# MLA latents normed in one step and transposed by feature tile, mask rows with their zeros in one transfer

## The chip, the cores and the metric

The kernel runs on one NeuronCore of a Trainium2 chip. The metric is the device time of one execution in microseconds, the median of the runs shown. The names of engines in rows are PE (TensorE, matmuls) and PEld (its weight loads), DVE (VectorE), ACT (ScalarE), POOL (GpSimd) and SP (SyncE, which issues most transfers). Each engine works through its own queue of instructions in a fixed order and stops at an instruction whose inputs or buffers are not ready.

## What is computed

One layer of a streaming encoder on 512 tokens of width 1024. The input is normed and multiplied with `w_in`; the result feeds two mixers, a Mamba-2 scan (16 heads in 4 groups) and a multi-head latent attention (MLA, 16 heads). Their outputs go through `w_out`; a cross-attention to 256 memory tokens and a convolutional feed-forward block follow, and a final norm. The part that the change touches is the way from the latents to the attention:

```python
q_lat, kv_lat, k_rope = jnp.split(u, [384, 640], axis=-1)          # u: 512 x 672
q  = (rmsnorm(q_lat,  q_norm_w)  @ w_q_up ).reshape(b, s, 16, 96)  # 64 plain, 32 rotary
kv = (rmsnorm(kv_lat, kv_norm_w) @ w_kv_up).reshape(b, s, 16, 128) # 64 key, 64 value
k_rope = apply_rope(k_rope, cos, sin)
mask = k_chunk[None, :] <= q_chunk[:, None]                        # chunks of 64 tokens
```

## The kernel before

Tokens are tiled by 128, so there are four token tiles `t`. All matrix products run as three matmuls in float32r: operands are split into a high part and a residue (`split`: a cast on ScalarE, line 94, and a subtraction on VectorE, line 95; weight pages use lines 156 to 158, where GpSimd takes half of the residue), and `mm3` (lines 103 to 105) adds high x high, high x low and low x high in one PSUM bank. PSUM has three `acc` banks for products, two `tr` banks for transposes, two `s` banks and one `pv` bank.

`lat` holds, for each token tile, 16 columns of dt, 384 of q latents, 256 of kv latents and 32 of rotary key. Its first 256 columns are made at the start; `late_unit(t)` makes the other 432 for one token tile, copying the accumulator to `lat` on ScalarE (line 674).

The scan goes through `seq`, 16 pairs of head group and token tile, in three steps: `ssd_a` (decay matrix aE, its transfer from DRAM on GpSimd's queue, line 537, the masked C-B product `cbm`, line 541, and the split of M and xs), `ssd_b` (products, state S, output y, its own norm) and `ssd_d` (transposes of y). For the last head group the steps are written out as strings in `PLAN`, one for each token tile. Its letters: z, d, a, b are the gate unit and the scan's steps, l a late unit, i `lat_init`, q0 to q3 and k0 to k3 the norms of q and kv latents of one token tile, p1 to p3 one to three output parts, U the first q projection (`q_up`), s and S the set-up of the key and query tiles.

A norm, `lat_norm`, squares the latents of one tile on ScalarE with a row sum (line 619), scales the sum on VectorE (line 140), raises it to the power -0.5 on GpSimd (line 142), multiplies latents, this factor and the weight row into a buffer of its own on VectorE (line 621), transposes three or two 128x128 blocks on TensorE into one `tr` bank (line 119) and splits each block into the tiles `LT[k]` (shown as `lt` in rows; lines 94 and 95). `lat_kv` also rotates the tile's rotary key in four steps on VectorE (lines 635 to 638). `q_up` multiplies `LT[0]` to `LT[2]` with a page of `w_q_up`, copies to `qrow` (line 723) and rotates there in four products on GpSimd (lines 726 to 729); `v_up` and `k_pair` use `LT[3]` and `LT[4]`.

An output part (`out_part`, lines 646 to 660) is a 256-column product of the scan's finished half with `w_out`, 12 matmuls; it reads rows of x into one of five `xo` buffers and writes the sum to DRAM. Sixteen such parts need no latents; those not named in `PLAN` run inside the attention loop as fills. `setup_kq1` (lines 685 to 693) fills the four mask rows of the key and query tiles: a memset for the low half and a transfer on GpSimd's queue for the high half.

The program is built through a planner (`schedule_with_timeline_sim=True`): it takes the order in which the code is written as priority, orders the instructions of each engine by a simulated timeline and adds the waits. The order on an engine is then fixed, and it need not be the order of the code.

Of the kernel before, what the change touches and what calls it, by code (L numbers as in the profile page):

```python
# [11 lines left out]
ALU = mybir.AluOpType  # L12
# [19 lines left out]
FM = FF // P  # L32
MASK_NEG = -float(2 ** 100)

PLAN = ('z z z z d a l l b', 'l l d a i q0 k0 p1 q1 b p1 q2 k1 p1 q3 k2', 'p1 d a k3 p1 b p1', 'p1 d U p2 b p3 s S')


def shape_constants():
    t = np.arange(P)[:, None]
    l = np.arange(P)[None, :]  # L40
    cen = ((t > 63) & (t <= l)).astype(np.float32) - ((t > l) & (t <= 63))
    c = np.concatenate([t == l, t <= l, cen, t <= l, t > l, np.ones((P, P))], axis=1).astype(np.float32)
    m = np.zeros((NT, 2, T), np.float32)
    for j in range(NT):
        m[j, 0, j * P:j * P + 64] = 1.0
        m[j, 1, j * P + 64:(j + 1) * P] = MASK_NEG
    f = np.array([np.float32(1.0) / np.float32(np.float64(10000.0) ** np.float64(np.float32(i) / np.float32(ROPE)))
                  for i in range(0, ROPE, 2)], np.float32).reshape(1, ROPE // 2)
    return c, m, f
# [13 lines left out]
def tile_block(ctx, tc, x, mem, positions, norm_mix_w, w_in, ssd_conv_w, ssd_conv_b, ssd_dt_bias,  # L63
# [541 lines left out]
    def lat_init():  # L605
        LT.extend(k4([P, 2, T], "lt", F32R) for _ in range(3))
        LT.extend(page("lt") for _ in range(2))
        qkl = k4([P, 1024], "qkl")
        box["qw"], box["kvw"] = row_tile(qkl[:, 0:QR], mla_q_norm_w), row_tile(qkl[:, QR:QR + KVR], mla_kv_norm_w)
        box["ln"] = qkl[:, QR + KVR:]  # L610
        nc.vector.tensor_scalar(box["qw"], box["qw"], float(QH) ** -0.5, None, ALU.mult)
        x4 = k4([P, 4, 256], "xo")
        xo.extend(x4[:, i] for i in range(3))
        box["lnk"] = [gw[0], x4[:, 3]]

    def lat_norm(t, o, n, w, l0, l1, ln):
        ss = small([P, 1], "ssl", 2)
        src = lat[:, t, SSD_H + o:SSD_H + o + n]
        nc.scalar.activation(ln, src, AF.Square, accum_out=ss)
        rs = rstd_of(ss, n, "l")  # L620
        nc.vector.scalar_tensor_tensor(ln, src, rs, w, ALU.mult, ALU.mult)
        ps = tr_bank().rearrange("p (k t) -> p k t", k=4)
        for k in range(l0, l1):
            transpose(ps[:, k - l0], ln[:, tsl(k - l0)])
        for k in range(l0, l1):
            split(LT[k][:, 0, tsl(t)], LT[k][:, 1, tsl(t)], ps[:, k - l0])

    def lat_q(t):
        lat_norm(t, 0, QR, box["qw"], 0, 3, box["ln"])

    def lat_kv(t):
        lat_norm(t, QR, KVR, box["kvw"], 3, 5, box["lnk"][t % 2])
        kr = lat[:, t, SSD_H + QR + KVR:]
        tmp = small([P, ROPE], "krt", 1)
        nc.vector.tensor_tensor(tmp[:, 0:H2], kr[:, H2:], sinb[:, t, 0:H2], ALU.mult)
        nc.vector.tensor_tensor(tmp[:, H2:], kr[:, 0:H2], sinb[:, t, H2:], ALU.mult)
        nc.vector.tensor_tensor(kr, kr, cosb[:, t], ALU.mult)
        nc.vector.tensor_tensor(kr, kr, tmp, ALU.add)

    with tc.issue_after(last):  # L640
        for u, rows in xbc_units(0):
# [23 lines left out]
    def late_unit(t):  # L665
        n, c0 = LATW - 256, C_DT + 256
        if t == 0:
            late_pages.extend(wpage(w_in[0][2 * P * j:2 * P * (j + 1), c0:c0 + n].rearrange(
                "(k p) c -> p k c", p=P), 2, n) for j in range(4))
        acc = acc_bank()[:, :n]  # L670
        for k in range(KD):
            hi, lo = late_pages[k // 2]
            mm3(acc, (hT[0][:, k, tsl(t)], hT[1][:, k, tsl(t)]), (hi[:, k % 2], lo[:, k % 2]), k == 0, k == KD - 1)
        nc.scalar.copy(lat[:, t, 256:], acc)

    late = [lambda t=t: late_unit(t) for t in range(NT)]
    parts = [lambda i=i: out_part(0, i) for i in range(16)]
# [7 lines left out]
    def setup_kq1():  # L685
        for b in range(2):
            kt = k4([P, 2, T], f"kt{b}", F32R)
            qt = k4([P, 2, T], f"qt{b}", F32R)
            for i, (tl, w) in enumerate(((qt, masks[:, 0]), (kt, masks[:, 1]))):
                nc.vector.memset(f32(tl[QH:KROWS, 1]), 0.0)  # L690
                nc.gpsimd.dma_start(tl[QH:KROWS, 0], w)
            kts.append(kt)
            qts.append(qt)

# [142 lines left out]
    def do(op, i):  # L837
        g, c = seq[i]
        if op == "z":
            z_unit(g, zn.pop(0))  # L840
        elif op == "l":
            late.pop(0)()
        elif op == "d":
            ssd_d(*seq[i - 1])
        elif op == "a":
            ssd_a(*seq[i + 1])
        elif op == "b":
            ssd_b(g, c)
        elif op == "i":
            lat_init()  # L850
        elif op[0] == "q":
            lat_q(int(op[1]))
        elif op[0] == "k":
            lat_kv(int(op[1]))
        elif op[0] == "p":
            part(int(op[1]))
        elif op == "s":
            setup_kq1()
        elif op == "U":
            q_up(0)  # L860
        elif op == "S":
            setup_kq2()
# [364 lines left out]
```

## Time and profile before

| | us |
|---|---|
| median of 3 runs (987.09 to 988.03) | 987.62 |
| profiled execution | 987.27 |
| its span, first to last instruction | 985.5 |
| TensorE busy | 965.7 |
| VectorE busy | 662.1 |
| ScalarE busy | 523.4 |
| GpSimd busy | 279.6 |
| mean granted TensorE clock | 0.994 |

All rows come from one profiled execution. A busy time adds up the time in which an engine has an instruction running, so it says nothing on whether the time that is left hurts: for that, the stretches and waits of the engine that is busiest are read, here TensorE's. A granted clock of 1 is 2.4 GHz.

### The profile page before, as it was taken

The numbers are of one execution on the slowest core, as the hardware profiler recorded it, in microseconds if no ns is written. First come the engines' busy times: TensorE is split into PE (matmuls) and PEld (weight loads), VectorE is DVE, ScalarE is ACT, GpSimd is POOL, SyncE is SP. The second block draws the span as 40 slices with busy tenths as digits, with TensorE's granted clock in tenths as the row PEclk, the third lists the DMA queues.
The fourth block names the chain that finished last, engine by engine and source line by source line (L and its number), as shares of the span: only waits on it lengthen the run. The fifth ranks groups of instructions, "written<-read, shape, count | busy, mean of one in ns | idle before, by whom it ended". The sixth has DMA issues, their size and how long they took to land.

```text
span 985.5 us, 14980 instructions
## 1 busy us (share of the span) xinstructions
PE 965.7 (98%) x5385; PEld 843.0 (86%) x5385; DVE 662.1 (67%) x1210; ACT 523.4 (53%) x1078; POOL 279.6 (28%) x360
## 2 busy tenths in 40 slices
PE   8999999999999999999999999999999999999997
PEld 6889998898899999988888888888888888888886
DVE  5989999868779786773654435766667666722553
ACT  5677776655477677753544434444444444321442
POOL 2016547656653547452443222000000000000000
PEclk9999999999999999999999999999999999999999
DMA  7653432315423336242241120433223322332462
GB/s 242 208 175 95 116 108 77 97 49 179 155 78 103 113 113 233 86 155 80 86 150 65 65 86 22 128 107 107 86 87 108 105 85 93 113 116 97 156 223 80
DMA packets 90306, 114.07 MB, mean 116 GB/s; under 512 B 5799, under 2 KB 70119, under 8 KB 89848
## 3 DMA queue, kind: packets, MB, share of 16 engines
q1 hardware_dynamic: 88536, 106.78, 34.0%
q0 software_dynamic: 1696, 6.33, 2.1%
q8 instruction: 43, 0.70, 0.3%
q14 instruction: 31, 0.25, 0.1%
HBM read 104.67 MB, written 8.42 MB: 115 GB/s over the span
## 4 chain that ended last, share of the span: by engine, by line
PE 82%; DVE 7%; DMA 3%; ACT 3%; POOL 2%; issue 2%; SPq 0%; POOLq 0%; ACTq 0%; DVEq 0%
PE acc L103 22%; PE acc L105 22%; PE acc L104 22%; PE tr L119 3%; PE s L103 3%; PE s L105 3%; PE s L104 3%; PE pv L811 2%; DMA aE<-acT 2%; DVE wl L157 1%; ACT aE L544 1%; PE acc L119 1%; DVE cu L434 1%; DMA wr<-in_w_in_dram 1%; POOL xdD L550 1%
## 5 line engine op out<-in xcount | busy, mean ns | idle before, releaser
L103 PE MATMUL acc<-Ah,wh 128*128 128x512 f32 (+1 forms) x560 | 215.5, 385 | 0.2 <-ACT Ah L94 0.2
L104 PE MATMUL acc<-Al,wh 128*128 128x512 f32 (+1 forms) x560 | 215.4, 385 | 0.2 <-DVE Al L95 0.2
L105 PE MATMUL acc<-Ah,wl 128*128 128x512 f32 (+1 forms) x560 | 215.0, 384 | 0.0
L95 DVE TENSOR_TENSOR wl<-wr,wh 128x1024 fp32r<-128x1024 f32 (+1 forms) x99 | 120.0, 1213 | 101.6 <-ACT wh L94 100.9
L94 ACT CAST wh<-wr 128x1024 fp32r<-128x1024 f32 (+1 forms) x99 | 102.0, 1031 | 133.5 <-PE acc L104 63.7
L158 POOL TENSOR_TENSOR wl<-wr,wh 128x512 fp32r<-128x512 f32 (+2 forms) x64 | 103.5, 1625 | 86.2 <-ACT wh L156 79.8
L142 POOL TENSOR_TENSOR rs<-ms,neg_half 128x1 f32<-128x1 f32 x18 | 10.8, 600 | 409.5 <-DVE ms L140 397.9
L104 PEld LDWEIGHTS acc<-Al,wh 128*128 128x128 f32 x560 | 105.3, 188 | 20.3 <-DVE Al L95 0.5
L105 PEld LDWEIGHTS acc<-Ah,wl 128*128 128x128 f32 x560 | 105.3, 188 | 20.2
L103 PEld LDWEIGHTS acc<-Ah,wh 128*128 128x128 f32 x560 | 105.2, 188 | 20.0 <-ACT Ah L94 0.5
L156 ACT CAST wh<-wr 128x1024 fp32r<-128x1024 f32 (+2 forms) x64 | 65.4, 1029 | 40.1 <-PE s L105 10.7
L1121 DVE SCALAR_TENSOR_TENSOR cbuf<-acc,fcw,cbuf 128x511 f32<-128x511 f32 (+1 forms) x88 | 65.6, 747 | 26.6 <-ACT cbuf L1119 25.1
L157 DVE TENSOR_TENSOR wl<-wr,wh 128x512 fp32r<-128x512 f32 (+2 forms) x64 | 59.3, 932 | 35.7 <-ACT wh L156 34.7
L103 PE MATMUL acc<-wh,Ah 128*128 128x256 f32 (+2 forms) x240 | 77.2, 323 | 1.0 <-ACT Ah L94 1.0
L105 PE MATMUL acc<-wh,Al 128*128 128x256 f32 (+2 forms) x240 | 76.2, 319 | 0.0
L104 PE MATMUL acc<-wl,Ah 128*128 128x256 f32 (+2 forms) x240 | 75.9, 318 | 0.0
L795 POOL TENSOR_SCALAR p<-p,ri 128x128 f32<-128x128 f32 (+1 forms) x64 | 34.5, 542 | 71.7 <-DVE ri L794 71.1
L103 PEld LDWEIGHTS acc<-wh,Ah 128*128 128x128 f32 x240 | 46.1, 192 | 4.2 <-ACT Ah L94 1.4
L105 PEld LDWEIGHTS acc<-wh,Al 128*128 128x128 f32 x240 | 46.1, 192 | 2.6 <-DVE Al L95 0.3
L104 PEld LDWEIGHTS acc<-wl,Ah 128*128 128x128 f32 x240 | 46.2, 192 | 2.3
L1119 ACT ACTIVATE cbuf<-acc,fcb,fcw 128x512 f32<-128x512 f32 x44 | 34.3, 779 | 24.0 <-PE acc L105 24.0
L104 PE MATMUL acc<-wl,act 128*128 128x512 f32 (+1 forms) x112 | 40.5, 363 | 0.0
(370 smaller groups left out, 2349.3 us busy)
## 6 DMA issues: line engine op xcount, KB each, us to landing
wr<-in_w_ffn_up_dram SPq DMA_DIRECT2D x44, 512.0 KB, 3.5
wr<-in_w_ffn_down_dram SPq DMA_DIRECT2D x33, 512.0 KB, 3.3
wr<-in_w_in_dram SPq DMA_DIRECT2D x26, 512.0 KB, 3.9
wr<-in_w_out_dram SPq DMA_DIRECT2D x16, 512.0 KB, 3.5
aE<-acT POOLq DMA_DIRECT2D x16, 256.0 KB, 3.5
wr<-in_w_mem_k_dram SPq DMA_DIRECT2D x8, 512.0 KB, 4.5
wr<-in_w_mem_v_dram SPq DMA_DIRECT2D x8, 512.0 KB, 3.4
wr<-in_w_mem_q_dram SPq DMA_DIRECT2D x8, 512.0 KB, 3.6
```

The costliest lines, as they stand in the source:

```text
L94: first = nc.scalar.copy(hi, src)
L95: nc.vector.tensor_tensor(lo, src, f32(hi), ALU.subtract)
L103: nc.tensor.matmul(acc, lhsT=lh, rhs=rh, start=first, stop=False)
L104: nc.tensor.matmul(acc, lhsT=lh, rhs=rl, start=False, stop=False)
L105: nc.tensor.matmul(acc, lhsT=ll, rhs=rh, start=False, stop=last)
L119: nc.tensor.transpose(dst, src, ident[:n, :n])
L156: nc.scalar.copy(hi, raw)
L157: nc.vector.tensor_tensor(lo[:, 0:a // 2], raw[:, 0:a // 2], f32(hi[:, 0:a // 2]), ALU.subtract)
L158: nc.gpsimd.tensor_tensor(lo[:, a // 2:], raw[:, a // 2:], f32(hi[:, a // 2:]), ALU.subtract)
L795: nc.gpsimd.tensor_scalar(p_, p_, ri, 1.0, ALU.mult, ALU.mult)
L1119: nc.scalar.activation(u, acc, AF.Identity, scale=fcw[:, 2, m:m + 1], bias=fcb[:, m:m + 1])
L1121: nc.vector.scalar_tensor_tensor(u[:, s:], acc[:, :T - s], fcw[:, 2 - s, m:m + 1], u[:, s:], ALU.mult, ALU.add)
```

## The change

The latents' norm is one step `n` for all four token tiles. The squares move into `late_unit`, write their (unused) squares into the accumulator bank just copied from, and collect their eight row sums in one small tile `lss`; `n` scales the eight sums in two operations, takes one power on GpSimd, multiplies the latents in place in `lat`, and rotates all four tiles' keys in four operations. The transposes are steps `t0` to `t4`, one for each feature tile: four 128x128 blocks, one per token tile, into one bank, and one split of 512 columns. The buffers of the scaled latents go; `xo` gets a sixth buffer. The plan names one output part less. The masks carry the zero half, so the four memsets go and each transfer writes both halves. The space for descriptors of GpSimd's transfers is set to 8192 bytes per partition.

```diff
--- before.py
+++ after.py
@@ -32,7 +32,7 @@
 FM = FF // P
 MASK_NEG = -float(2 ** 100)
 
-PLAN = ('z z z z d a l l b', 'l l d a i q0 k0 p1 q1 b p1 q2 k1 p1 q3 k2', 'p1 d a k3 p1 b p1', 'p1 d U p2 b p3 s S')
+PLAN = ('z z z z d a l l b', 'l l d a i n b p1 t0 p1 t1 t2', 'p1 d a t3 p1 t4 b p1', 'p1 d U p2 b p3 s S')
 
 
 def shape_constants():
@@ -40,10 +40,10 @@
     l = np.arange(P)[None, :]
     cen = ((t > 63) & (t <= l)).astype(np.float32) - ((t > l) & (t <= 63))
     c = np.concatenate([t == l, t <= l, cen, t <= l, t > l, np.ones((P, P))], axis=1).astype(np.float32)
-    m = np.zeros((NT, 2, T), np.float32)
+    m = np.zeros((NT, 2, 2, T), np.float32)
     for j in range(NT):
-        m[j, 0, j * P:j * P + 64] = 1.0
-        m[j, 1, j * P + 64:(j + 1) * P] = MASK_NEG
+        m[j, 0, 0, j * P:j * P + 64] = 1.0
+        m[j, 1, 0, j * P + 64:(j + 1) * P] = MASK_NEG
     f = np.array([np.float32(1.0) / np.float32(np.float64(10000.0) ** np.float64(np.float32(i) / np.float32(ROPE)))
                   for i in range(0, ROPE, 2)], np.float32).reshape(1, ROPE // 2)
     return c, m, f
@@ -607,35 +607,35 @@
         LT.extend(page("lt") for _ in range(2))
         qkl = k4([P, 1024], "qkl")
         box["qw"], box["kvw"] = row_tile(qkl[:, 0:QR], mla_q_norm_w), row_tile(qkl[:, QR:QR + KVR], mla_kv_norm_w)
-        box["ln"] = qkl[:, QR + KVR:]
         nc.vector.tensor_scalar(box["qw"], box["qw"], float(QH) ** -0.5, None, ALU.mult)
         x4 = k4([P, 4, 256], "xo")
-        xo.extend(x4[:, i] for i in range(3))
-        box["lnk"] = [gw[0], x4[:, 3]]
-
-    def lat_norm(t, o, n, w, l0, l1, ln):
-        ss = small([P, 1], "ssl", 2)
-        src = lat[:, t, SSD_H + o:SSD_H + o + n]
-        nc.scalar.activation(ln, src, AF.Square, accum_out=ss)
-        rs = rstd_of(ss, n, "l")
-        nc.vector.scalar_tensor_tensor(ln, src, rs, w, ALU.mult, ALU.mult)
-        ps = tr_bank().rearrange("p (k t) -> p k t", k=4)
-        for k in range(l0, l1):
-            transpose(ps[:, k - l0], ln[:, tsl(k - l0)])
-        for k in range(l0, l1):
-            split(LT[k][:, 0, tsl(t)], LT[k][:, 1, tsl(t)], ps[:, k - l0])
-
-    def lat_q(t):
-        lat_norm(t, 0, QR, box["qw"], 0, 3, box["ln"])
-
-    def lat_kv(t):
-        lat_norm(t, QR, KVR, box["kvw"], 3, 5, box["lnk"][t % 2])
-        kr = lat[:, t, SSD_H + QR + KVR:]
-        tmp = small([P, ROPE], "krt", 1)
-        nc.vector.tensor_tensor(tmp[:, 0:H2], kr[:, H2:], sinb[:, t, 0:H2], ALU.mult)
-        nc.vector.tensor_tensor(tmp[:, H2:], kr[:, 0:H2], sinb[:, t, H2:], ALU.mult)
-        nc.vector.tensor_tensor(kr, kr, cosb[:, t], ALU.mult)
+        xo.extend(x4[:, i] for i in range(4))
+
+    lss = small([P, 2 * NT], "lss", 1)
+
+    def lat_norm():
+
+        rs = small([P, 2 * NT], "lrs", 1)
+        for i, n in enumerate((QR, KVR)):
+            h = slice(i * NT, (i + 1) * NT)
+            nc.vector.tensor_scalar(lss[:, h], lss[:, h], 1.0 / n, EPS, ALU.mult, ALU.add)
+        nc.gpsimd.tensor_tensor(rs, lss, neg_half.broadcast_to([P, 2 * NT]), ALU.pow)
+        for t in range(NT):
+            for i, (o, n, w) in enumerate(((SSD_H, QR, "qw"), (SSD_H + QR, KVR, "kvw"))):
+                v = lat[:, t, o:o + n]
+                nc.vector.scalar_tensor_tensor(v, v, rs[:, i * NT + t:i * NT + t + 1], box[w], ALU.mult, ALU.mult)
+        kr = lat[:, :, SSD_H + QR + KVR:]
+        tmp = small([P, NT, ROPE], "krt", 1)
+        nc.vector.tensor_tensor(tmp[:, :, 0:H2], kr[:, :, H2:], sinb[:, :, 0:H2], ALU.mult)
+        nc.vector.tensor_tensor(tmp[:, :, H2:], kr[:, :, 0:H2], sinb[:, :, H2:], ALU.mult)
+        nc.vector.tensor_tensor(kr, kr, cosb, ALU.mult)
         nc.vector.tensor_tensor(kr, kr, tmp, ALU.add)
+
+    def lat_T(k):
+        ps = tr_bank()
+        for t in range(NT):
+            transpose(ps[:, tsl(t)], lat[:, t, SSD_H + P * k:SSD_H + P * (k + 1)])
+        split(LT[k][:, 0], LT[k][:, 1], ps)
 
     with tc.issue_after(last):
         for u, rows in xbc_units(0):
@@ -672,6 +672,8 @@
             hi, lo = late_pages[k // 2]
             mm3(acc, (hT[0][:, k, tsl(t)], hT[1][:, k, tsl(t)]), (hi[:, k % 2], lo[:, k % 2]), k == 0, k == KD - 1)
         nc.scalar.copy(lat[:, t, 256:], acc)
+        for i, (o, m) in enumerate(((SSD_H, QR), (SSD_H + QR, KVR))):
+            nc.scalar.activation(acc[:, 0:m], lat[:, t, o:o + m], AF.Square, accum_out=lss[:, i * NT + t:i * NT + t + 1])
 
     late = [lambda t=t: late_unit(t) for t in range(NT)]
     parts = [lambda i=i: out_part(0, i) for i in range(16)]
@@ -686,9 +688,8 @@
         for b in range(2):
             kt = k4([P, 2, T], f"kt{b}", F32R)
             qt = k4([P, 2, T], f"qt{b}", F32R)
-            for i, (tl, w) in enumerate(((qt, masks[:, 0]), (kt, masks[:, 1]))):
-                nc.vector.memset(f32(tl[QH:KROWS, 1]), 0.0)
-                nc.gpsimd.dma_start(tl[QH:KROWS, 0], w)
+            for i, tl in enumerate((qt, kt)):
+                nc.gpsimd.dma_start(tl[QH:KROWS], masks[:, i])
             kts.append(kt)
             qts.append(qt)
 
@@ -848,10 +849,10 @@
             ssd_b(g, c)
         elif op == "i":
             lat_init()
-        elif op[0] == "q":
-            lat_q(int(op[1]))
-        elif op[0] == "k":
-            lat_kv(int(op[1]))
+        elif op == "n":
+            lat_norm()
+        elif op[0] == "t":
+            lat_T(int(op[1]))
         elif op[0] == "p":
             part(int(op[1]))
         elif op == "s":
@@ -1211,7 +1212,7 @@
     import concourse.bacc as _bacc
     from concourse.bass_utils import run_bass_kernel_spmd as _run
 
-    nc = _bacc.Bacc("TRN2", target_bir_lowering=False, num_devices=1)
+    nc = _bacc.Bacc("TRN2", target_bir_lowering=False, num_devices=1, dynamic_dma_scratch_size=8192)
     arrays, args = {}, []
     named = [(n, np.ascontiguousarray(inputs[n])) for n in _INS]
     named[-1] = ('norm_final_w', named[-1][1].reshape(1, D))
```

## Rows read from the trace of the kernel before

**Rows 1.** The page's busy times: busy us (share of span) x instructions.

```profile
PE 965.7 (98%) x5385; PEld 843.0 (86%) x5385; DVE 662.1 (67%) x1210; ACT 523.4 (53%) x1078; POOL 279.6 (28%) x360
```

**Rows 2.** Table of stretches: stretch, its length, each engine's busy us (count), clock, DMA.

```profile
270.00:620.00 350.00, 349.77 (x2090) 311.15 (x2088) 223.71 (x484) 201.18 (x499) 144.40 (x184) 1.00 0.32 104
```

**Rows 3.** Table of stretches, the two dips and two 5 us at a lower clock.

```profile
215.00:230.00 15.00, 12.89 (x78) 11.98 (x78) 12.10 (x30) 8.07 (x19) 9.89 (x11) 0.89 0.31 99
225.00:230.00 5.00, 4.82 (x29) 4.61 (x28) 5.00 (x16) 2.69 (x9) 1.58 (x2) 0.66 0.79 249
240.00:250.00 10.00, 7.40 (x42) 5.47 (x41) 7.36 (x22) 4.47 (x20) 7.71 (x15) 1.00 0.49 159
250.00:255.00 5.00, 5.00 (x28) 5.00 (x29) 3.99 (x12) 1.99 (x6) 3.85 (x8) 0.66 0.12 33
```

**Rows 4.** TensorE's waits, 195 to 275 us: total us, times, longest.

```profile
PE tr L119 <- DVE lt L95: 2.1, 1, 2.1
PE s L103 <- DVE cbm L541: 1.2, 1, 1.2
```

**Rows 5.** Timeline of TensorE: start, us, instruction, idle before and releaser.

```profile
224.33 0.39 PE L103 MATMUL s<-xs,Br 128*128 128x256 f32 x1 [1.15 <-DVE cbm L541]
...
238.52 0.34 PE L103 MATMUL acc<-wh,lt 128*128 128x384 f32 x1
...
248.97 0.55 PE L119 MATMUL tr<-cst,qkl 128*128 128x128 f32 x3 [2.08 <-DVE lt L95]
```

**Rows 6.** Timeline of VectorE (DVE).

```profile
221.08 2.99 DVE L157 TENSOR_TENSOR wl<-wr,wh 128x512 fp32r<-128x512 f32 x2 [0.26 <-ACT wh L156]
224.00 0.28 DVE L541 TENSOR_TENSOR cbm<-s,cst 128x128 f32<-128x128 f32 x1
...
244.55 0.43 DVE L140 TENSOR_SCALAR msl<-ssl 128x1 f32<-128x1 f32 x2
...
247.64 0.62 DVE L621 SCALAR_TENSOR_TENSOR qkl<-lat,rsl,qkl 128x384 f32<-128x384 f32 x1 [2.17 <-POOL rsl L142]
...
260.36 0.27 DVE L95 TENSOR_TENSOR lt<-tr,lt 128x128 fp32r<-128x128 f32 x1
```

**Rows 7.** Timeline of GpSimd (POOL).

```profile
220.18 4.76 POOL L158 TENSOR_TENSOR wl<-wr,wh 128x512 fp32r<-128x512 f32 x3 [0.20 <-ACT wh L156]
...
243.15 1.45 POOL L726 TENSOR_TENSOR rt<-qrow,sinb 128x64 f32<-128x64 f32 x1
...
247.06 1.05 POOL L142 TENSOR_TENSOR rsl<-msl,neg_half 128x1 f32<-128x1 f32 x2
```

**Rows 8.** Groups by shape, 200 to 262 us: count, busy us, mean ns, idle before.

```profile
L95 DVE TENSOR_TENSOR lt<-tr,lt 128x128 fp32r<-128x128 f32 x20 | 5.4, 280 | 0.1
...
L621 DVE SCALAR_TENSOR_TENSOR qkl<-lat,rsl,qkl 128x384 f32<-128x384 f32 x4 | 2.4, 612 | 2.4 <-POOL rsl L142 2.4
...
L95 DVE TENSOR_TENSOR M<-aE,M 128x512 fp32r<-128x512 f32 x3 | 2.0, 682 | 0.4 <-ACT M L94 0.4
...
L621 DVE SCALAR_TENSOR_TENSOR gw<-lat,rsl,qkl 128x256 f32<-128x256 f32 x2 | 1.0, 478 | 0.0
...
L142 POOL TENSOR_TENSOR rsl<-msl,neg_half 128x1 f32<-128x1 f32 x8 | 4.3, 544 | 3.5 <-DVE msl L140 3.5
```

**Rows 9.** Timeline of ScalarE (ACT).

```profile
210.07 1.28 ACT L544 ACTIVATE aE<-aE,cenT 128x128 f32<-128x128 f32 x4 [3.51 <-DMA aE<-acT]
211.26 0.51 ACT L619 ACTIVATE qkl<-lat 128x384 f32<-128x384 f32 x1
...
212.08 0.18 ACT L619 ACTIVATION_READ_ACCUMULATOR gw<-lat 128x1 f32 x1
...
221.69 0.50 ACT L674 COPY lat<-acc 128x432 f32<-128x432 f32 x1
```

**Rows 10.** Line 635's instructions: count, ns min/median/max, first and last start, shape.

```profile
L635 DVE TENSOR_TENSOR krt<-lat,sinb x4: 169/190/772, 206.9 to 224.2; 128x16 f32<-128x16 f32 x4
```

## The prediction, made before the change was run

> **What bounds the kernel now.** I read the page's busy times first: TensorE is busy for 98% of the span [rows 1], so only its idle time and the time it spends at the lower clock can be won. The table of stretches says where these are. From 270 to 620 us TensorE lacks 0.23 us in 350 [rows 2]: there the change can win nothing, only harm. The stretch that it rewrites, 205 to 262 us (the last head group's scan, the MLA latents and the first output parts), has two dips. In the first, 215 to 230 us, TensorE lacks 15.00 - 12.89 = 2.1 us; in the second, 240 to 250 us, 10.00 - 7.40 = 2.6 us [rows 3]. At the end of the first and right after the second the mean granted clock of 5 us is 0.66 [rows 3]: with two levels, 2.4 and 1.2 GHz, that is 3.4 us at the lower one, and 5 x 0.34 = 1.7 us of work lost. So dip one costs 3.8 us and dip two 4.3 us.
>
> TensorE's waits of the stretch name what ended the two longest stops [rows 4], and the timelines of three engines side by side tell why. *Dip two:* TensorE starts again at 248.97, after 2.08 us, with the transposes of the fourth token tile's q latents [rows 5]; the list puts the wait down to VectorE's lt, line 95. VectorE itself had stood 2.17 us until 247.64 for `rsl`, the power -0.5 on GpSimd [rows 6]. The power's inputs were written by 244.98 [rows 6], and GpSimd was not idle: from 243.15 it worked through six products (four of the rope of the first q projection, one gate product y, one xdD sum) and came to the power at 247.06 [rows 7]. So the chain is GpSimd's queue, the scaling on VectorE, the transposes; and it exists because the norm goes tile by tile, so that the rope of earlier tiles is queued when tile 3 is still to be normed. *Dip one:* its largest stop, 1.15 us, is for cbm, line 541 [rows 5], which stood behind two weight residues, line 157, that took 2.99 us together [rows 6] while GpSimd ran three of its own, line 158, from 220.18 to 224.94 [rows 7]. That is not the latents' work.
>
> **The change, part by part.** *Norm in one step.* Eight powers on GpSimd, 8 x 0.544 = 4.3 us [rows 8], become one on 128x8. The 128x1 form bounds it below at 0.54; the longest 128x64 product here, 1.45 us [rows 7], above; I take 0.55, since the form is nearest. What matters is its place: it has to come before any q projection, so no rope can be queued ahead of it. That takes away dip two's chain: 2.6 us of idle and the 1.7 us behind it, 4.3 us. The eight scalings stay (4 x 0.612 + 4 x 0.478 = 4.4 us [rows 8]), but six of them move forward, from 228.9 to 249.4 us to some 225 us, right behind the fourth latent product. I cost them at zero; what hides them is the output parts, which need no latents and which the planner already puts ahead of the first q projection (238.52 [rows 5]); without that cover they cost up to their 4.4 us. New waits: VectorE's first scaling waits for the power, and the power for the last row sum. Behind them in VectorE's queue stand cbm, S and y of the scan, for which TensorE waits.
>
> *Row sums in the latent step.* The eight squares on ScalarE move from ahead of each norm to behind each copy of line 674 and write into the accumulator's bank. The pair of squares and their two reads took from 211.26 to 212.26, 1.0 us [rows 9], so a bank is held 1.0 us longer. The fourth copy ran at 221.69 [rows 9], so that bank would come free at 223.2 instead of 222.2. Three banks rotate, so two further products stand before it is wanted. Cost: zero, at most 1.0 us.
>
> *Transposes by feature tile.* 20 before and after: nothing on TensorE. Twenty residues of 128 columns, 5.4 us on VectorE, become five of 512 (0.682, as M's), 3.4 us [rows 8]; ScalarE's casts shrink likewise, and the two tr banks are taken five times instead of eight. *Rope of the key rows:* sixteen small operations on VectorE become four, 128x64 or 128x128 (nearest row: cbm, 0.28 [rows 6]), 1.1 us. *Masks:* four memsets go from VectorE; the four transfers remain, each with twice the bytes, and land long before the first score. All of this shortens engines that do not bound the kernel, so I count it as 0, between -1 (dip one's VectorE queue gets shorter) and 0.
>
> *The smaller descriptor space of GpSimd's transfers.* No row shows GpSimd waiting for it. Below it is 0; above, one wait such as ScalarE's 3.51 us for an aE transfer [rows 9]. I take 0, as the kernel has some 22 such transfers and they stand microseconds apart.
>
> *One part fewer ahead of the attention loop, six row buffers for parts instead of five.* The part moves into the loop, where TensorE is full either way: 0.
>
> Sum: -4.3 us. Against the profiled execution, 987.27 us (span 985.5 and 1.8 around it), that is 983.0. The median of the runs is 0.35 above the profiled one, so 983.3.
>
> What is late next once dip two is gone: TensorE is 4 us earlier at the value projection, whose last operand, line 95's lt, was written at 260.36 to 260.6 [rows 6]. That residue belongs to the latents too and will be done earlier, with the step t4. Its weights and the rope products of tile 3 remain; see the third rival.
>
> **The rivals.** *The merged norm stands in the way (slower).* Each engine's order is fixed when the program is built. If dip one's cbm is queued behind the scalings, it waits for the power, and that for GpSimd's three residues: 224.94 + 0.55 = 225.5; then 4.4 us of scalings and 1.1 of key rope, so cbm at 231.0 instead of 224.0 [rows 6]: 7.0 us more idle against the 4.3 gained, 987.27 + 2.7 = 990.0, or 990.3 on the median's scale. It costs more than it gains from the point at which five of the eight scalings stand ahead of cbm (1.5 + 5 x 0.55 = 4.3). For it: VectorE is full from 225 to 230 us [rows 3], and the block is moved to just there. Against: cbm belongs to step `a`, ahead of `n` in the plan, and needs nothing of the fourth latents, whose copy starts at 221.69.
>
> *GpSimd slows the scalings (same).* Operations with two inputs in SBUF took longer beside line 158: a weight residue 1.5 us where M's, of the same width, took 0.682 [rows 6, 8], and a step of the key rope 0.772 where its median is 0.190 [rows 10]. If each of the eight scalings took 0.9 us more, the q latents would be ready at 225.5 + 4.4 + 1.1 + 7.2 + 2.0 (three 512-wide residues) = 240.2, where the first q projection ran at 238.52 [rows 5]: 1.7 us of idle and again 1.7 at the lower clock, 983.3 + 3.4 = 986.7. For it: the block is moved to where those residues run. Against: they ended at 224.94, before the power can. The Trainium skill, page "SBUF — State Buffer", section "Who interferes with whom", says that VectorE and GpSimd share a pair of SBUF ports, and that a VectorE instruction with two SBUF inputs contends with a GpSimd instruction that reads SBUF, the later one being blocked whole. By that rule every scaling beside a GpSimd product could be held up for as long as that product runs. The rows on the residue and on krt agree in direction.
>
> *Something else takes dip two's place (same).* The stop may come back at the next wait, on the rope products (GpSimd is busy for 77% of 240 to 250 us [rows 3]) or on weights: 986 to 987.6.
>
> *Both dips go.* With VectorE's small steps fewer the planner may set cbm earlier: 983.3 - 3.8 = 979.5.
>
> **How the numbers follow.** Forecast 0.50, both dips 0.12, slowed scalings 0.14, another wait 0.10, slower 0.14. What a measurement of this kernel can tell from no change is about 0.2%, 2 us: faster 0.62, same 0.24, slower 0.14. The range reaches from both dips gone, 979.2, to the near edge of the slower case, 988.9; most of that case's 0.14 lies above it.
>
> **What would show it.** Right: between 235 and 255 us no wait of TensorE over 0.5 us and a granted clock of 1.0; one power `lrs` on GpSimd ahead of every rope product; five 512-wide residues for lt; no stop from 270 to 620 us. Wrong: TensorE waiting between 220 and 240 us for cbm, lt or transposes of lat; scalings of over 1 us; a long gap of VectorE until the power; or the parts ending before the latents are ready, so that TensorE runs dry.

## The result: slower by 1.8%

The changed kernel takes 1006.09 us (median of 4 runs, 1004.11 to 1006.45) where the kernel before takes 987.83 us in the same batch: ratio 1.018, 95% interval 1.0162 to 1.0197, 18.3 us slower. The prediction was 983.3 us with a range of 979.2 to 988.9.

First the page's busy times of the changed kernel, the line of [rows 1] (engine, busy us, share of the span, instructions):

```profile
span 1002.3 us, 14890 instructions
...
PE 971.2 (97%) x5385; PEld 845.5 (84%) x5385; DVE 664.2 (66%) x1173; ACT 522.4 (52%) x1063; POOL 279.1 (28%) x353
```

TensorE has the same 5385 matmuls. It is idle for 1002.3 - 971.2 = 31.1 us where it was idle for 19.8 [rows 1], and busy 5.5 us longer for the same work, which is what a lower clock looks like. Next where: stretches of the changed kernel (stretch, its length, TensorE busy and its instructions, granted clock, share of the DMA engines, GB/s), the first line for [rows 2], the next for [rows 3].

```profile
270.00:620.00 350.00, 341.88 (x2031) 0.99 0.33 106
...
220.00:240.00 20.00, 14.65 (x106) 0.91 0.41 131
240.00:260.00 20.00, 18.85 (x106) 0.74 0.36 114
260.00:280.00 20.00, 19.01 (x148) 1.00 0.55 168
280.00:300.00 20.00, 18.45 (x118) 1.00 0.26 83
...
380.00:400.00 20.00, 14.43 (x84) 0.83 0.78 270
400.00:420.00 20.00, 20.00 (x163) 1.00 0.18 54
```

The same stretches of the kernel before:

```profile
220.00:240.00 20.00, 18.46 (x132) 0.91 0.52 169
240.00:260.00 20.00, 17.40 (x109) 0.91 0.39 121
260.00:280.00 20.00, 19.78 (x151) 1.00 0.53 172
280.00:300.00 20.00, 20.00 (x137) 1.00 0.30 88
...
380.00:400.00 20.00, 19.98 (x151) 1.00 0.41 128
```

Two places carry the loss. From 220 to 300 us TensorE is busy for 70.96 us instead of 75.64, 4.7 us more idle, and 20 x (1 - 0.74) + 20 x 0.09 = 7.0 us of work go to the lower clock instead of 3.6: 8.1 us in all. From 380 to 400 us, far behind everything that the change rewrites, it is idle for 5.6 us and loses 20 x 0.17 = 3.4 to the clock: 9.0 us. Together that is 17.1 us, where the spans differ by 16.8.

**The first place.** GpSimd and VectorE of the changed kernel, the lines for [rows 7] and [rows 6] (start, us, instruction, idle before and releaser):

```profile
228.45 2.23 POOL L622 TENSOR_TENSOR lrs<-lss,neg_half 128x8 f32<-128x8 f32 x1 [0.64 <-DVE lss L621]
```

```profile
220.70 0.69 DVE L157 TENSOR_TENSOR wl<-wr,wh 128x512 fp32r<-128x512 f32 x1 [4.07 <-ACT wh L156]
...
231.35 4.80 DVE L626 SCALAR_TENSOR_TENSOR lat<-lat,lrs,qkl 128x384 f32<-128x384 f32 x8
236.07 0.41 DVE L95 TENSOR_TENSOR S<-S 128x256 fp32r<-128x256 f32 x1
236.41 0.28 DVE L541 TENSOR_TENSOR cbm<-s,cst 128x128 f32<-128x128 f32 x1
...
236.94 0.68 DVE L157 TENSOR_TENSOR wl<-wr,wh 128x512 fp32r<-128x512 f32 x1
```

The power runs at 228.45, not at the 225 that I had put down, and VectorE then does all eight scalings in one block of 4.80 us. Behind the block stand the state's residue S, the next cbm and the residue of a `w_out` page (line 157). SyncE's queue shows what hangs on the last one:

```profile
237.68 0.38 SPq L148 DMA_DIRECT2D wr<-in_w_out_dram  x1
238.11 1.93 SPq L654 DMA_DIRECT2D xo<-in_x_dram  x4
```

The next `w_out` page is asked for at 237.68, after 3.3 us of waiting for a residue of line 157, and the rows of x for the next parts behind it in the same queue. So the output parts, which I had named as the cover of the scalings, themselves wait for VectorE. TensorE's three longest stops from 233.5 to 246 us:

```profile
234.88 0.44 PE L119 MATMUL tr<-cst,lat 128*128 128x128 f32 x2 [0.75 <-DVE lat L626]
...
239.30 1.09 PE L119 MATMUL tr<-cst,lat 128*128 128x128 f32 x4 [1.32 <-DVE lt L95]
...
241.46 0.58 PE L104 MATMUL s<-S,bc 128*128 128x256 f32 x1 [0.85 <-DVE S L95]
```

No single stop is long, against [rows 4] (2.1 and 1.2 us), but there are many in a row, and the clock follows, at half its speed while TensorE is full:

```profile
245.00:250.00 5.00, 5.00 (x24) 0.50 0.33 104
```

Dip two as it was is gone: no rope stands ahead of the power. The first score starts at 271.64 us instead of 266.68.

**The second place.** VectorE and GpSimd of the changed kernel near 388 us:

```profile
388.43 4.34 DVE L157 TENSOR_TENSOR wl<-wr,wh 128x512 fp32r<-128x512 f32 x1
...
393.17 0.87 DVE L95 TENSOR_TENSOR PT<-tr,PT 128x256 fp32r<-128x256 f32 x2
```

```profile
387.33 0.84 POOL L728 TENSOR_TENSOR rt<-qrow,sinb 128x64 f32<-128x64 f32 x1
388.11 1.18 POOL L828 DMA_DIRECT2D memT<-memT_d  x2
389.31 1.29 POOL L158 TENSOR_TENSOR wl<-wr,wh 128x512 fp32r<-128x512 f32 x1
390.55 0.45 POOL L729 TENSOR_TENSOR qrow<-qrow,cosb 128x128 f32<-128x128 f32 x1
390.96 1.26 POOL L158 TENSOR_TENSOR wl<-wr,wh 128x512 fp32r<-128x512 f32 x1
```

The memory's transposed rows, memT, 2 MB, are asked for at 388.11, and a weight residue that takes 0.69 us elsewhere lasts 4.34; TensorE stands 3.48 us until 393.72 for the residue PT behind it, and its first product with memT follows at 394.76:

```profile
393.72 1.39 PE L119 MATMUL tr<-cst,p 128*128 128x128 f32 x5 [3.48 <-DVE PT L95]
394.76 0.56 PE L103 MATMUL acc<-memT,wh 128*128 128x256 f32 x1
```

In the kernel before the same transfer is issued, and the first product with memT runs, here:

```profile
365.71 1.21 POOL L827 DMA_DIRECT2D memT<-memT_d  x2 [3.78 <-PE s L784]
```

```profile
375.85 0.36 PE L103 MATMUL acc<-memT,wh 128*128 128x256 f32 x1
```

The reason can be read in the code. memT takes the buffer of yS, which every output part reads, so its load starts only when the last part has run. In the kernel before the last part's last matmul starts at 365.25, and TensorE goes on with the rest of a head and the last q projection; the first product with memT runs at 375.85. In the changed kernel one more part is left for the loop, whose slots are counted (`fill_count`): the last part comes one slot later, behind that projection (385.20), and the product with memT is next.

### The profile page after: what moved, and what is told of

It is laid out like the page before. It is cut to its first block, busy times and chain, and to the rows that moved or that the text cites. A ratio compares the mean times of both kernels' runs of the same rounds, so it can differ in the third digit from the quotient of the medians.

```text
span 1002.3 us, 14890 instructions
## 1 busy us (share of the span) xinstructions
PE 971.2 (97%) x5385; PEld 845.5 (84%) x5385; DVE 664.2 (66%) x1173; ACT 522.4 (52%) x1063; POOL 279.1 (28%) x353
## 4 chain that ended last, share of the span: by engine, by line
PE 82%; DVE 8%; ACT 3%; issue 3%; POOL 2%; DMA 2%; SPq 0%; POOLq 0%; DVEq 0%; ACTq 0%
PE acc L103 22%; PE acc L105 22%; PE acc L104 22%; PE tr L119 3%; PE s L104 2%; PE s L105 2%; PE s L103 2%; PE pv L812 2%; DMA aE<-acT 1%; DVE wl L157 1%; ACT wh L156 1%; DVE cu L434 1%; DVE wl L95 1%; DMA wr<-in_w_in_dram 1%; PE acc L119 1%
## 5 line engine op out<-in xcount | busy, mean ns | idle before, releaser
L158 POOL TENSOR_TENSOR wl<-wr,wh 128x512 fp32r<-128x512 f32 (+2 forms) x64 | 101.0, 1587 | 83.9 <-ACT wh L156 80.1
L157 DVE TENSOR_TENSOR wl<-wr,wh 128x512 fp32r<-128x512 f32 (+2 forms) x64 | 65.0, 1021 | 42.4 <-ACT wh L156 42.2
L796 POOL TENSOR_SCALAR p<-p,ri 128x128 f32<-128x128 f32 (+1 forms) x64 | 37.1, 581 | 84.7 <-DVE ri L795 76.7
```

What stands on the lines that cost most here:

```text
L157: nc.vector.tensor_tensor(lo[:, 0:a // 2], raw[:, 0:a // 2], f32(hi[:, 0:a // 2]), ALU.subtract)
L158: nc.gpsimd.tensor_tensor(lo[:, a // 2:], raw[:, a // 2:], f32(hi[:, a // 2:]), ALU.subtract)
L796: nc.gpsimd.tensor_scalar(p_, p_, ri, 1.0, ALU.mult, ALU.mult)
```

## The experiments

Theory for the second place: the part taken out of the plan moves memT's load past its cover. Theory for the first: the block of scalings puts the norm's VectorE work ahead of the scan's. Rivals: the power's length; transposes by feature tile; the squares' place; the masks and the descriptor space.

**One part less, in the kernel before.** `e1_before_one_part_less`, nothing else changed:

```diff
-b p1 q2 k1 p1 q3 k2'
+b p1 q2 k1 q3 k2'
```

> The kernel before with one output part fewer ahead of the attention loop (the last p1 of the second string is left out), nothing else. Theory A (the fill list of the loop, longer by one part, brings the loop's stops): most of the 9.6 us that the changed kernel loses between 270 and 420 us shows here, 994 to 998 us, with a stop of VectorE's weight residue beside GpSimd. Theory B (the merged norm and its place bring everything): the part moves into a full TensorE, 986.5 to 989 us.

1001.45 us, ratio 1.0139 (1.0124 to 1.0155): 13.8 us for one part, with nothing of the norm touched, and more than either theory gave. Its stretch and its transfer:

```profile
380.00:400.00 20.00, 13.83 (x72) 0.74 0.61 219
```

```profile
381.64 1.21 POOL L827 DMA_DIRECT2D memT<-memT_d  x2
```

The same residue lasts 4.36 us at 381.96. This run does not yet say whether the slot costs this or the work missing ahead of the loop.

**The slot alone.** In `e10_last_fill_one_slot_later` stage 1 is as before, with all its parts; the loop's first head gives one slot less. In `e9_one_part_less_and_a_slot_more` the part is missing and a slot more makes up for it.

```diff
# e10
-return int(i < 0 or qi == 1 or (qi == 0 and i > 3))
+return int(i < 0 or (qi == 1 and i != 0) or (qi == 0 and i > 3))
# e9, e11
+return int(i < 0 or qi == 1 or (qi == 0 and (i > 3 or i == 0)))
```

> The kernel before with stage 1 untouched and one fill taken out of the loop's first head, so that every later fill stands one slot later and the last output part in head 10, first query tile, right ahead of the first product with memT. If the load of memT behind that part is the cause of e1's loss: TensorE stops between 380 and 400 us at a low clock (about 14 busy of 20), memT's transfers are issued 10 us or more later than 365.7, and the time is 996 to 1002. If the cause is the work that was missing ahead of the loop, that work is there: 987 to 989.5.

> The kernel before with one output part less ahead of the loop (as e1_before_one_part_less) and one fill more in the loop's first head, so that the last output part stands in the same slot as in the kernel before (head 9, second query tile) and only an early place differs. If e1's 13.8 us come from the load of memT, which can start only when the last output part has let go of its buffer and then has the very next slot behind it: memT's transfers are issued near 362 to 366 us again, the VectorE residue of 4.36 us and the stop at 380 to 400 are gone, and the time is 985.5 to 989. If e1's loss comes from too little work ahead of the loop, or from the thinner start of it, the part that is missing there is still missing: 997 to 1001.5.

e10: 998.39 us, ratio 1.0104 (1.0085 to 1.0123), with memT issued at 380.14. e9: 990.47 us, ratio 1.0024 (1.0013 to 1.0035), with memT issued at 369.46 and 380 to 400 us full. So the slot costs 10 us by itself, and 11 of e1's 13.8 us come back when the slot does; the 2.4 us that stay lie with the part's earlier place or with the slot that was added in the first head, which these runs do not separate. e9 ends above the 985.5 to 989 that I gave it. The stretch of e10, with 5.5 us idle and 5.2 lost at the clock, holds that whole loss:

```profile
380.00:400.00 20.00, 14.51 (x84) 0.74 0.60 196
```

**The same in the changed kernel.** `e11_changed_and_a_slot_more` has e9's slot; `e6_after_with_part_back` has the part back in the plan (`t0 p1 t1 p1 t2`).

> The changed kernel, stage 1 untouched, with the same fill more in the loop's first head. If the loss of the changed kernel at 380 to 400 us is the slot of its last output part: that stretch is full again at clock 1.0, and the time is 995.5 to 999, near e6_after_with_part_back (997.47), with the losses of 220 to 260 us as in the changed kernel. If it is the work missing ahead of the loop: 1003 to 1006.5.

> The changed kernel with the output part put back ahead of the attention loop (one p1 more in the second string, between t1 and t2): norm, transposes, masks and space as changed. Theory A (the missing part shifts the loop's fills, so that memT and the first page of w_mem_k meet the last q projection's rope on GpSimd): the 4.34 us residue and the stop at 385 to 395 us are gone, TensorE lacks under 1 us from the first score to 420 us, and the time is 989 to 994 us, what is left over 987.7 being the first stage's loss. Theory B (the merged norm disturbs the loop too): over 998 us.

995.41 us, ratio 1.0067 (1.005 to 1.0084), and 997.47, ratio 1.0091 (1.0074 to 1.0108). In both 380 to 400 us is full at clock 1.0. About half of the loss, 8.6 to 10.7 us, was the slot. The time of e6 lies between the two that I gave; what it still loses is mostly in the first stage.

**Is it GpSimd's share of the weight split?** `e8_memk_pages_without_gpsimd` takes GpSimd's halves out of the residues of the `w_mem_k` pages.

> The changed kernel, eleven parts, with the pages of w_mem_k split without GpSimd's half (VectorE does the whole residue, some 1.2 us a page). Theory A1 (the stop at 385 to 395 us is VectorE held up by GpSimd's queue of residues and rope): no VectorE operation over 2.5 us there, the 5.6 us of idle and 1.7 us of low clock shrink by 5 to 7 us, to 998 to 1002 us. Theory A2 (the stop comes from memT's transfers, late as they are): the stop stays within 1.5 us, 1004 to 1007 us.

1004.33 us, ratio 1.0158 (1.0143 to 1.0173). No residue is long there any more, and the stop stays, now with memT among the waits:

```profile
380.00:400.00 20.00, 15.33 (x78) 0.74 0.77 269
```

```profile
PE s L103 <- DVE p L788: 1.7, 1, 1.7
PE acc L103 <- DMA memT<-memT_d: 1.6, 1, 1.6
```

So the long residue is not what makes the stop. That the 2 MB and the weight pages come when the product that needs them is next fits e8 to e11 and the code. No run gave memT a buffer of its own, so which of the transfers that come late there sets the stop is argued, not shown; that the slot costs it is shown.

**One part more.** If the slot's price is lost cover, more cover should gain nothing. `e16_before_one_part_more` (`q3 p1 k2`) and `e17_four_powers_one_part_more` (the same on e14, below) have 13 parts ahead of the loop instead of 12.

> The kernel before with one output part more ahead of the loop (13 in place of 12), so that the last output part, and with it memT's load, comes one slot earlier than in the kernel before (head 9, first query tile). If the loss of e1 is the load of memT without cover, more cover than the load needs gains nothing: 986.5 to 989. If it is a general price of about 10 us for every part that is not ahead of the loop: below 982.

> e14_four_powers_into_scratch (four powers ahead of the ropes, scaled into the old scratch buffers) with 13 output parts ahead of the loop. If the stops that e14 has left at 220 to 240 us (2.5 us) and at 300 to 320 (1.0 us) lack work for TensorE, a part more gives back up to 1.4 us: 986 to 987.5. If they are VectorE's backlog, which a part's own sum makes longer, nothing: 987.5 to 989.

992.31 us, ratio 1.0046 (1.0031 to 1.0061), and 993.51, ratio 1.0059 (1.0042 to 1.0076): both slower, against what I expected. The stretches of e16:

```profile
360.00:380.00 20.00, 18.29 (x122) 1.00 0.44 154
...
420.00:620.00 200.00, 197.81 (x986) 1.00 0.27 87
```

The first product with memT is now one slot earlier too and runs at 370.58, ahead of the last projection, after 0.48 us of waiting for memT, so these two runs did not give the load the cover that I had meant to test; and 420 to 620 us, which the kernel before fills to 199.89, lacks 2.2. The order before is better than one slot later and than one part more. Which of the shifted fills costs the 2.2 us was not tried.

**The masks and the descriptor space.** `e2_before_masks_and_space` makes these two edits in the kernel before.

> The kernel before with the mask rows and their zeros in one transfer, without the four memsets, and with the descriptor space of 8192 bytes; norms and plan as before. Theory C (the smaller space slows GpSimd's transfers, the two of memT above all): over 990 us, with longer transfers of aE and memT. Theories A and B: 986.5 to 988.5 us, the two dips of the kernel before unchanged.

988.59 us, ratio 1.0006 (0.9997 to 1.0016): no difference that the runs can tell.

**The power.** `e5_without_power` leaves out the power, with a reciprocal on VectorE in its place; the orders of the engines are otherwise those of the changed kernel.

> The changed kernel with the power -0.5 of the eight row sums, 2.23 us on GpSimd, replaced by a reciprocal on VectorE, some 0.15 us (the factors are then not those of the norm). The orders of all engines stay the same but for that row. Theory B1 (the power's length holds the block up): the block starts 1 to 2.5 us earlier and the time falls by 2 to 4 us, to 1002 to 1004 us. Theory B2 (VectorE was working without a gap until the block anyway, so its backlog sets the start): the first score moves by under 1 us, 1004.5 to 1006.5 us.

1005.51 us, ratio 1.0179 (1.0164 to 1.0195). The scalings start at 232.20, 6.85 us behind the start of the cbm, where the changed kernel has 6.79 (231.35 and 224.56), though nothing on GpSimd is waited for. VectorE's queue sets their start, and the power's 2.23 us lie beside it.

**The block against pieces.** `e4_norm_by_tile` replaces `n` by `n0 n1 n2 n3`: four powers of 128x2, and two scalings behind each. `e7_by_tile_with_part_back` is e4 with the part back.

```diff
-nc.gpsimd.tensor_tensor(rs, lss, neg_half.broadcast_to([P, 2 * NT]), ALU.pow)
-for t in range(NT):
+nc.gpsimd.tensor_tensor(lrs[:, c], lss[:, c], neg_half.broadcast_to([P, 2]), ALU.pow)
```

> The changed kernel with the norm taken token tile by token tile (four powers of 128x2 and two scalings behind each, at the place of the single step), in place and with the transposes by feature tile as they are. Theory B (the block of eight scalings behind one power stands in VectorE's queue ahead of the scan's S and the weight residue, and TensorE runs dry): four to six scalings move into VectorE's idle time from 210 to 221 us, the first score comes 3 to 5 us earlier than at 271.6, and the time falls to 1000 to 1003 us, further if the loop's stops go too. If not the block but the transposes by feature tile are the cause (the first q projection waits for all tiles): 1004 to 1007 us.

> As the run with the part put back, but with the norm token tile by token tile (four powers of 128x2). With the loop out of the way this pair measures the block of scalings alone. If the block behind the one power costs the first stage: 2 to 4 us less than the run with the part put back. If not: within 1 us of it.

1003.86 us, ratio 1.0165 (1.015 to 1.018), and 991.37, ratio 1.0039 (1.0027 to 1.005). Pieces save 2.2 us where the part is missing, a time between the two that I gave, and 6.1 where it is in place (e6 against e7), where I had given 2 to 4. In the profile of e4 the first place is some 4 us better than in the changed kernel, and the second 2.5 us worse (13.76 us busy at clock 0.74 from 380 to 400 us), which hides part of the saving. e7 shows dip two's stretch as the prediction wanted it, and a new stop behind it:

```profile
235.00:240.00 5.00, 3.29 (x29) 1.00 0.75 218
240.00:245.00 5.00, 5.00 (x37) 1.00 0.63 203
245.00:250.00 5.00, 5.00 (x36) 1.00 0.39 120
250.00:255.00 5.00, 5.00 (x45) 1.00 0.40 123
255.00:260.00 5.00, 4.62 (x34) 1.00 0.46 132
260.00:265.00 5.00, 2.88 (x19) 0.84 0.88 268
```

**The rest, step by step from the kernel before.** e15 moves the squares alone. e12 to e14 have before's plan and transposes by token tile, squares in the late step, and all powers ahead of the first rope (one step `n` before `q0`): e12 eight powers of 128x1 and scaling in place; e13 four of 128x2, in place; e14 as e13, but scaled into the old scratch buffers.

```diff
# e13 against e14
-ln = lat[:, t, SSD_H + o:SSD_H + o + n]
+src = lat[:, t, SSD_H + o:SSD_H + o + n]
-nc.vector.scalar_tensor_tensor(ln, ln, lrs[:, c:c + 1], w, ALU.mult, ALU.mult)
+nc.vector.scalar_tensor_tensor(ln, src, lrs[:, c:c + 1], w, ALU.mult, ALU.mult)
```

> The kernel before with only the squares moved into the late step (into the step's accumulator bank); powers one by one where they were, behind the ropes, scaling into the scratch buffers, masks as before. If the squares' place costs nothing, dip two stays and the time is 987 to 989. If the squares hold the late step's bank and ScalarE so that the sums of the next part come late, TensorE loses more at 222 to 232 than before (3.5 us there now) and the time is 989.5 to 992.

> The kernel before with its plan and its transposes by token tile, and of the change only the squares in the late step, the scaling in place, and the powers: all eight (128x1 each) on GpSimd ahead of the first rope. The masks are as before. If dip two (the clock's 3.4 us at 250 and the wait for a power behind the rope at 244 to 248) costs what the prediction says and what e7_by_tile_with_part_back gives back comes from the transposes by feature tile (all ropes, masks and weight splits in one bunch near 250): TensorE is full from 235 to 255 at clock 1.0, nothing new stops it to 320, and the time is 982.5 to 985. If instead the squares in the late step or the powers' row of eight (about 4.4 us of GpSimd ahead of the first scaling) make the norm late, the first scalings wait near 228 to 232 and the time is 987 to 992.

> As e12_powers_first_by_token_tile, but four powers of 128x2 (0.7 us each, 2.8 in all) in place of eight of 128x1 (6.67 us in all). If the length of the row of powers is what made e12 late, GpSimd is free 3.9 us earlier and the time falls to 987.5 to 990. If what made it late is the scalings that go ahead of the masked product on VectorE, little changes: 990.5 to 993.

> As e13, but scaled into the scratch buffers of the kernel before, which a scaling gets only when the transposes of an earlier tile have read them; the powers still stand ahead of the ropes. If the old buffers kept the order of VectorE right (a scaling per tile, other work between) and the powers' early place removes dip two: 982.5 to 985.5, TensorE full from 240 to 255 at clock 1.0. If scaling in place has nothing to do with it: no better than e13 by over 1 us.

e15: 988.14 us, ratio 1.0004 (0.9993 to 1.0015). e14: 987.94, ratio 1.0001 (0.999 to 1.0013). e13: 989.56, ratio 1.0015 (1.0003 to 1.0028). e12: 992.67, ratio 1.0038 (1.0023 to 1.0053). e12 ends above both of its ranges, and e14 well above the 982.5 to 985.5 of its first.

The row of powers of e12 takes 6.67 us, and the half of a weight residue that GpSimd owes comes behind it:

```profile
228.49 6.67 POOL L624 TENSOR_TENSOR lrs<-lss,neg_half 128x1 f32<-128x1 f32 x8
235.14 1.48 POOL L158 TENSOR_TENSOR wl<-wr,wh 128x512 fp32r<-128x512 f32 x1
```

Four powers of two columns save 3.1 us of e12's time. Scaling into the scratch buffers saves 1.6 more, which is not clear of the measurement's 0.2%: in e14 the scalings stand apart again, between the scan's steps, since a buffer is free only when an earlier tile has been transposed. And e14 tests the prediction's main term, the early powers, with the plan and the transposes as before.

```profile
220.00:240.00 20.00, 17.49 (x128) 0.91 0.50 159
240.00:260.00 20.00, 18.87 (x133) 1.00 0.50 153
260.00:280.00 20.00, 19.49 (x147) 1.00 0.48 155
280.00:300.00 20.00, 19.82 (x133) 1.00 0.32 100
300.00:320.00 20.00, 18.97 (x136) 1.00 0.20 61
```

From 240 to 260 us it gains 18.87 - 17.40 = 1.5 us busy and 1.8 at the clock, 3.3 in all. It loses 1.0 at 220 to 240, 0.3 and 0.2 in the next two, and 0.9 at 300 to 320, where the kernel before has 19.91. The total does not move.

But e15, which moves the squares alone and was expected to leave dip two as it was, has more than half of that gain:

```profile
240.00:260.00 20.00, 17.72 (x121) 1.00 0.42 128
```

That is 0.3 us more busy than the kernel before and 1.8 at the clock. Its longest stop there is 0.77 us, where the kernel before has 2.08, and its last power for the latents runs at 243.74, just ahead of the first rope product at 244.26. So early row sums by themselves bring the powers ahead of the rope, with the norm still tile by tile, and the total does not move here either. These clocks are those of one execution each: over the 25 executions of the kernel before beside e13 to e15 the mean granted clock goes from 0.992 to 0.998, and the time from 991.32 to 985.79 us, so that a gain of 1.8 us at the clock in one of them is no more than what one execution differs from the next. No kernel here beat the kernel before.

## Why the prediction was wrong

**"One part fewer ahead of the attention loop: 0."** This step failed first, and is worth 8.6 to 10.7 us (e6, e11) in the changed kernel. I wrote that TensorE is full in the loop either way. [rows 2] showed that for the order of before; I read a property of the loop from it. I costed the part's 1.4 us of matmuls and not its place: it shifts every later fill by a slot, and what hangs on the last of them is a transfer of 2 MB whose buffer it frees. A step that is moved takes along whatever is counted from it.

**"Eight scalings cost zero, at most 4.4 us."** The duration was nearly right: 4.80 us together. ([rows 8] shows two of the four narrow scalings of before; the other two took 0.57 us each, not 0.478.) The cover was wrong: e6 against e7 says 6.1 us for having them in one block behind one power, more than their own length. In the profiled executions 3.6 of the 5.3 us between the two spans are the lower clock and 1.9 are idle time from 260 to 280 us, where e6 waits 2.3 us for GpSimd's rope; so the price is that of the order which comes with the block, and not of the scalings alone. The parts that should have hidden them need VectorE themselves, for their weight residues and their sums, and their transfers wait in SyncE's order behind those pages. Work that needs the busy engine is no cover for that engine.

**"The power: 0.54 to 1.45, I take 0.55."** It took 2.23 us (1.66 in e8), beyond my upper bound; the rows had the power at one column only, and I took the price of one column for eight. It cost nothing that e5 could find, since VectorE was later.

**"It has to come before any q projection ... that takes away dip two's chain: 4.3 us."** The mechanism holds in part. In e14 the stretch from 240 to 260 us is at clock 1.0 and 1.5 us fuller, and in e7 the 15 us from 240 are full. But I wrote that the wait exists because the norm goes tile by tile, and in e15 it still does so: there the early squares are enough to bring the last power ahead of the rope, and the stop of 2.08 us is gone. The size does not hold: for the whole kernel the early powers are worth 0.1 us in e14, well within its interval. About 3.3 us come where I said, and others are lost in the stretches around it. Why 300 to 320 us then lacks a microsecond was not tried.

**The zeros that held.** Squares in the late step (e15, ratio 1.0004) and masks and descriptor space (e2, 1.0006) cost nothing beyond their intervals. Transposes by feature tile were not measured alone. From e13 to e7 they come together with the rope of all tiles, the masks and the plan's order, and the sum is 1.8 us.

So the 18.3 us can be stacked from medians: before 987.9; squares and early powers 987.9 (e14); in place 989.6 (e13); by feature tile, with the new plan 991.4 (e7); scalings in one block 997.5 (e6); a part less 1006.1. Only the last two steps are clear of the noise, and these are differences of an order that each step reshuffles, not prices that must add up elsewhere.

**The rivals.** "The merged norm stands in the way" had the mechanism of the first place, at 990.3 us and a chance of 0.14. The cbm that I named escaped: it ran at 224.56, ahead of the block, as I had argued against the rival. The next ones, S and the cbm of the following tile, did not. I had looked at the instruction that was late in the trace of before and not at all that the block would pass. "GpSimd slows the scalings" hardly happened: the four wide ones took 0.604 us each (0.612 before), and of the four narrow ones three took 0.47 (0.478 before) [rows 8] and one 1.50, beside GpSimd's weight residue from 232.45. That is 1.0 us in all where I priced 7.2. "Something else takes dip two's place" happened in e7 (260 to 265 us). "Both dips go" did not.

**What would show it.** No wait over 0.5 us and clock 1.0 from 235 to 255 us: no, 1.32 us at 239.30 and clock 0.50 from 245 to 250. One power ahead of every rope: yes. Five residues of 512 for lt: yes, 0.678 us each where I took 0.682. No stop from 270 to 620 us: no, 8.12 us are missing there. Of the signs for wrong, the waits for cbm, lt and lat at 220 to 240 us and TensorE running dry both came, and one scaling of over 1 us.

## What to carry to other kernels

When a step leaves a hand-written plan, count the slots behind it and find out which buffer the last of them frees and which transfer waits for that buffer; one slot was 10 us here, on an engine that the table showed full. Work covers for a busy engine only if it does not need that engine itself. Scaling in place takes away a buffer, and with it a wait that spaced the operations; that this lets them pass work which others need first was not shown clear of the noise (e13 against e14, 1.6 us).

## What the runs showed of the hardware

GpSimd's power takes longer with more columns: 0.54 us for 128x1 [rows 8], about 0.70 for 128x2 (the median of four in e4, the longest 1.15), 2.23 for 128x8 in the changed kernel, e6 and e11 and 1.66 in e8. So the width is not all that sets its length. Eight single ones in a row took 6.67 us (e12), from 0.54 to 1.23 each, and were dearer than one of eight columns.

A weight residue of VectorE that takes 0.69 us alone lasted 4.34 in the changed kernel, 4.36 in e1 and 4.37 in e10, always with GpSimd working without a gap beside it (387.33 to 392.22 in the rows above), and ended some 0.5 us after GpSimd's queue had. The Trainium skill, page "SBUF — State Buffer", section "Who interferes with whom", says that a VectorE instruction with two SBUF inputs contends with a GpSimd instruction that reads SBUF, and calls the pair of ports that they share an exclusive lock, with the order of issue deciding who is blocked. The trace agrees that the residue is held up, and shows more: it is held over a whole queue with a transfer's issue between, and three GpSimd instructions that start after it (389.31, 390.55 and 390.96) end before it. 3.65 us were added, where the longest single one took 1.29. e8 shows that this was not what set the end.
